# Wider dilated values, matmuls of one width in groups, an earlier first norm, row loads held in their place and five more warm-up matmuls in an fp32 encoder block

## The chip, the cores and the metric

The kernel runs on one core of one Trainium2 chip. The metric is the device time of one execution in microseconds (us). A core has a matmul engine (TensorE, PE in the profile; PEld is its weight load), two engines for elementwise work (VectorE, DVE; ScalarE, ACT), GpSimd (POOL), SyncE (SP) whose queue issues most transfers, and 16 DMA engines. Matmuls write eight accumulation banks of 128 partitions by 512 floats.

## The reference, cut to what matters

One encoder block over 256 tokens of width 2048, all in fp32:

```python
h = rms_norm(x, attn_norm)
qa, ka, va, qb, kb, vb, ga, gb = split(h @ w_in)           # A: 8 query heads, 2 key/value heads; B: 12 heads in 3 groups
ya = windowed_gqa(qa, ka, va, rel_bias_table, sink_a)       # |i-j| <= 128, a sink logit per head
yb = dilated_attention(qb, kb, vb, rel_bias_table)          # dilations 1, 4, 16; the groups merged by their denominators
merged = sigmoid(ga) * (ya @ w_branch_a) + sigmoid(gb) * (yb @ w_branch_b)
x = x + merged @ w_out
hf = rms_norm(x, ffn_norm)
g = dwconv_centred(hf @ w_ffn_gate, conv_w, conv_b)         # depthwise, width 3
x = x + (gelu(g) * (hf @ w_ffn_up)) @ w_ffn_down            # width 5632
x = x + sigmoid(rms_norm(x, ple_norm) @ w_ple_gate) * (p @ w_ple_proj)
return rms_norm(x, final_norm)
```

## The kernel before

**Precision.** Every matmul operand is held as a high and a low half (type fp32r). ACT writes a weight unit's high half (`uh`, L261, a copy that rounds), DVE its low half (`ul`, L262, the rest). The product is high x high, high x low and low x high. An activation tile such as `hs` (normed input) or `hf` (input of the MLP) holds per 128 channels a row of 512: 256 tokens high, 256 tokens low.

**Weights.** They come in pieces of 1 MB (`raw`, three buffers, SP's queue, L241). A piece is two units of 1024 columns, eight blocks of 128 x 128 each; six units of `uh` and `ul` exist. `drop` gives a unit back and `pump` then orders the next one's copies.

**Products.** Where the weights stand still in the array (`block`), one block costs a pair of matmuls: L289, the high half against all 512 columns, and L290, the low half against the 256 high columns, adding to the upper half of the same bank:

```python
nc.tensor.matmul(acc, hi[:, w], m, start=first, stop=False, skip_group_check=True)
nc.tensor.matmul(acc[:, T:], lo[:, w], m[:, :T], start=False, stop=last, skip_group_check=True)
```

`product` runs 16 such pairs, over 16 chunks of channels. Values must come with tokens on the partitions, so `value_product` has the activation stand still and the weights move: L312, L313, L314 per chunk and token half, over as many columns as heads are done at once (two heads: 256). All later stages but the MLP's first half (gates, branches, output, down projection, embedding) move 512 columns of weights, three matmuls at a time (L324 to L326), many in a Strassen form over "S" pieces.

**Order.** `_plan` lists the projections. The first seven (two keys, five queries of A) run interleaved, chunk by chunk, while weights and input arrive. Then come A's values (job FIRST = 7), three queries, and for each of four `j`: near values (dilation 1, two heads, every second `j`), three keys, far values (two heads), three queries. `at` hangs small work on (job, step) and `run_due` emits it in front of that step: with job i the last query of an attention block, scores at (i+1, 9), transposes at (i+2, 11 or 12), weighted values at (i+3, 4). The scores take the key and query tiles `kf`, `qf`, and for far heads `k`, `q` (L712). A compiler's scheduler orders the instructions of each engine from this program; `keep` fixes an instruction's place.

**The norm.** The projections work on the input without its norm; `rms` hangs up the sums of squares (L429), the root on DVE and POOL (L435, L437), the diagonal `rdg` (L444) and its broadcast by PE (L450), and everything behind a projection (`after`) multiplies by it. A second such norm stands in the MLP's first half.

**Start and rows.** Before the first product PE multiplies constants (`WARM` = 9). In the output projection's first stage, `D0`, the kernel loads the residual's rows `xr` (four loads of 0.5 MB, L870, on SP's queue) and transposes the last `merged` chunks (L812).

**The MLP.** Two halves, `E0` and `E1`, of 44 products each, gate and up in turn; the first four of `E0` run jointly. In `E0`, steps 2 to 5 transpose the residual into `hf`.

## Time and profile before

| | |
|---|---|
| median of 3 runs | 1474.07 us (1472.39 to 1474.58) |
| the profiled execution | 1474.83 us, of which the program's span is 1473.0 |
| PE busy | 1456.9 us, 7766 matmuls |
| PE weight load busy | 1247.8 us |
| DVE busy | 1241.5 us |
| ACT busy | 810.5 us |
| DMA | 282.93 MB, mean 192 GB/s |
| granted PE clock over the span | 0.998 |

A row of the timeline has start, duration, engine, source line, operation, output <- inputs, shape, count, and in brackets the idle time before it and what ended that. A row of the table by stretches has the stretch, its length, then for each engine the busy time with the number of instructions in brackets, the granted PE clock, the DMA share and GB/s. A matmul's duration reaches over the start of the next one, since matmuls are pipelined: what one costs in a stream is the distance between starts.

### The profile page before, as it was taken

How to read it: one execution, taken by the hardware profiler on the slowest of the kernel's cores; microseconds unless marked ns; L12 is line 12 of the kernel's file. 1: busy time of each engine (PE TensorE's matmuls, PEld its weight loads, DVE VectorE, ACT ScalarE, POOL GpSimd, SP SyncE). 2: the span in 40 equal slices, each digit the busy share in tenths (PEclk: the TensorE clock that was granted, in tenths of full speed). 3: DMA queues.
4: the chain of work that ended last, by engine and by line, in shares of the span. 5: the costliest groups of instructions: out<-in, count | busy, mean ns of one | idle time of the engine just before them, and what ended most of it. 6: DMA issues, size and time to landing. Idle time of an engine off the chain costs nothing.

```text
span 1473.0 us, 20121 instructions
## 1 busy us (share of the span) xinstructions
PE 1456.9 (99%) x7766; PEld 1247.8 (85%) x7766; DVE 1241.5 (84%) x1841; ACT 810.5 (55%) x1153; POOL 4.8 (0%) x9
## 2 busy tenths in 40 slices
PE   9999999999999999999999999999999999999997
PEld 8899999988888887888888888888888888888785
DVE  7587665669989989989888899988888889999994
ACT  7466444446555555565555556454555555555763
POOL 0000000000000000000000000000000000000000
PEclk9999999999999999999999999999999999999999
DMA  9654454445456456464555545465545455446462
GB/s 318 236 199 144 154 184 178 160 155 200 172 200 229 169 211 248 155 234 185 199 183 189 201 152 219 181 248 176 196 176 196 178 194 179 184 188 232 168 222 93
DMA packets 46460, 282.93 MB, mean 192 GB/s; under 512 B 5076, under 2 KB 9812, under 8 KB 14108
## 3 DMA queue, kind: packets, MB, share of 16 engines
q1 hardware_dynamic: 45356, 280.20, 52.1%
q10 hardware_dynamic: 1008, 1.45, 0.3%
q8 instruction: 61, 1.00, 0.3%
q14 instruction: 35, 0.29, 0.1%
HBM read 279.49 MB, written 2.14 MB: 191 GB/s over the span
## 4 chain that ended last, share of the span: by engine, by line
PE 91%; DVE 4%; DMA 2%; ACT 1%; issue 1%; POOL 0%; POOLq 0%; ACTq 0%
PE bank L289 31%; PE bank L290 15%; PE bank L324 12%; PE bank L325 12%; PE bank L326 12%; DMA raw<-in_wts 2%; PE bank L312 2%; PE bank L313 2%; PE bank L314 2%; DVE ul L262 1%; DVE vl L262 1%; ACT uh L261 1%; PE bank L812 1%; PE bank L635 0%; PE bank L582 0%
## 5 line engine op out<-in xcount | busy, mean ns | idle before, releaser
L261 ACT ACTIVATE uh<-raw 128x1024 fp32r<-128x1024 f32 (+2 forms) x518 | 522.6, 1017 | 493.1 <-PE bank L289 272.0
L262 DVE TENSOR_TENSOR ul<-raw,uh 128x1024 fp32r<-128x1024 f32 (+2 forms) x518 | 601.0, 1171 | 184.4 <-ACT uh L261 181.8
L289 PE MATMUL bank<-hf,uh 128*128 128x512 f32 x1408 | 493.6, 397 | 0.0
L290 PE MATMUL bank<-hf,ul 128*128 128x256 f32 x1408 | 393.4, 280 | 0.0
L289 PEld LDWEIGHTS bank<-hf,uh 128*128 128x128 f32 x1408 | 264.6, 188 | 63.1
L290 PEld LDWEIGHTS bank<-hf,ul 128*128 128x128 f32 x1408 | 265.7, 189 | 0.2
L289 PE MATMUL bank<-hs,uh 128*128 128x512 f32 x544 | 195.9, 402 | 2.1 <-DVE hs L422 2.1
L290 PE MATMUL bank<-hs,ul 128*128 128x256 f32 x544 | 153.5, 283 | 0.0
L261 ACT ACTIVATE vh<-raw 128x1024 fp32r<-128x1024 f32 x92 | 97.4, 1058 | 59.9 <-DVE raw L254 28.3
L289 PEld LDWEIGHTS bank<-hs,uh 128*128 128x128 f32 x544 | 103.5, 190 | 25.0 <-DVE hs L422 2.4
L262 DVE TENSOR_TENSOR vl<-raw,vh 128x1024 fp32r<-128x1024 f32 x92 | 112.2, 1221 | 0.5 <-ACT vh L261 0.2
L290 PEld LDWEIGHTS bank<-hs,ul 128*128 128x128 f32 x544 | 104.3, 192 | 0.1
L324 PE MATMUL bank<-uh,act 128*128 128x512 f32 x232 | 90.8, 391 | 0.0
L325 PE MATMUL bank<-ul,act 128*128 128x512 f32 x232 | 90.7, 391 | 0.0
L326 PE MATMUL bank<-uh,act 128*128 128x512 f32 x232 | 90.7, 391 | 0.0
L324 PE MATMUL bank<-uh,hs 128*128 128x512 f32 x172 | 67.6, 393 | 0.0
L326 PE MATMUL bank<-uh,hs 128*128 128x512 f32 x172 | 67.5, 392 | 0.0
L325 PE MATMUL bank<-ul,hs 128*128 128x512 f32 x172 | 67.3, 391 | 0.0
L312 PE MATMUL bank<-uh,hs 128*128 128x256 f32 x224 | 63.8, 285 | 0.0
L313 PE MATMUL bank<-ul,hs 128*128 128x256 f32 x224 | 63.5, 283 | 0.0
L314 PE MATMUL bank<-uh,hs 128*128 128x256 f32 x224 | 63.4, 283 | 0.0
L254 DVE TENSOR_TENSOR raw<-raw 128x1024 f32<-128x1024 f32 x46 | 56.2, 1222 | 0.5
(236 smaller groups left out, 2232.4 us busy)
## 6 DMA issues: line engine op xcount, KB each, us to landing
raw<-in_wts SPq DMA_DIRECT2D x251, 1024.0 KB, 4.8
raw<-in_wts SPq DMA_DIRECT2D x12, 512.0 KB, 6.7
xr<-in_xrow SPq DMA_DIRECT2D x4, 512.0 KB, 9.8
x<-in_xt SPq DMA_DIRECT2D x13, 128.0 KB, 5.8
hb<-hold SPq DMA_DIRECT2D x3, 514.0 KB, 7.6
hb<-hold SPq DMA_DIRECT2D x2, 768.0 KB, 6.6
last<-in_gainrow SPq DMA_DIRECT2D x1, 1024.0 KB, 4.8
out<-xr SPq DMA_DIRECT2D x4, 256.0 KB, 2.6
```

The costliest lines, as they stand in the source:

```text
L254: nc.vector.tensor_tensor(raw[:, :2 * WIDE], raw[:, WIDE:3 * WIDE], raw[:, :2 * WIDE], op=ALU.subtract)
L261: nc.scalar.activation(hi, src, AF.Copy)
L262: nc.vector.tensor_tensor(lo, src, hi.bitcast(F32), op=ALU.subtract)
L289: nc.tensor.matmul(acc, hi[:, w], m, start=first, stop=False, skip_group_check=True)
L290: nc.tensor.matmul(acc[:, T:], lo[:, w], m[:, :T], start=False, stop=last, skip_group_check=True)
L312: nc.tensor.matmul(acc[:, :T], xh, hi, start=(k == 0), stop=False)
L313: nc.tensor.matmul(acc[:, :T], xh, lo, start=False, stop=False)
L314: nc.tensor.matmul(acc[:, :T], xl, hi, start=False, stop=(k == KC - 1))
L324: nc.tensor.matmul(acc, sh, wh, start=first, stop=False)
L325: nc.tensor.matmul(acc, sh, wl, start=False, stop=False)
L326: nc.tensor.matmul(acc, sl, wh, start=False, stop=last)
L812: nc.tensor.transpose(p[:, k, t * P:(t + 1) * P], src(t)[:, k * P:(k + 1) * P], ident)
```

## The change

It does the following.

- Values of B: near values of all four heads in one product, far values of two `j` (four heads) in one product: 512 moving columns instead of 256. A's values stay at 256.
- Products behind the first seven take two units at a time: all high matmuls of the sixteen blocks, then all low ones (`unit_blocks`, `JOINED`). Work hung on a step is emitted among the high ones.
- The first norm's sums at step 4 and its broadcast at step 10 of A's values, instead of steps 6 and 12 of the query product behind.
- `WARM` 14 instead of 9.
- The four row loads keep their place in the program.
- `yb` becomes four tiles, whose room holds the far values first and part of the MLP's activations later; some small tiles have one buffer, `tb` shares one, `rd` is padded to 32 columns.

Line numbers of the changed kernel are higher: L289 and L290 are L305 and L309 in grouped products (L291 and L292 in the first seven), L261 and L262 are L263 and L264, L312 to L314 are L343 to L345, L581 to L583 are L612 to L614, L870 is L907.

PE, the query product behind A's values and the first scores (`bank` an accumulation bank, `uh`, `ul` a unit's halves). Before, the end of the product and the scores' start:

```order
L289 MATMUL bank_757<-hs_98,uh_582 128x512
L290 MATMUL bank_757<-hs_98,ul_583 128x256
L289 MATMUL bank_757<-hs_98,uh_610 128x512
L290 MATMUL bank_757<-hs_98,ul_611 128x256
L581 MATMUL bank_788<-kf_722,qf_730 128x256
L582 MATMUL bank_788<-kf_722,qf_730 128x256
```

And now:

```order
L309 MATMUL bank_693<-hs_102,ul_524 128x256 x8
L309 MATMUL bank_693<-hs_102,ul_528 128x256 x8
L305 MATMUL bank_761<-hs_102,uh_586 128x512 x8
L305 MATMUL bank_761<-hs_102,uh_626 128x512
L612 MATMUL bank_777<-kf_707,qf_715 128x256
L613 MATMUL bank_777<-kf_707,qf_715 128x256
L614 MATMUL bank_777<-kf_707,qf_715 128x256
```

The scores still stand in front of step 9, now behind nine high matmuls instead of nine pairs.

DVE, from the gathering of the first products (`first`) to the norm's root (`rv`). Before:

```order
L549 TENSOR_TENSOR rows_529<-bank_527,mk_102 20x512
L411 SCALAR_TENSOR_TENSOR first_534<-bank_148,t_535 128x256
L411 SCALAR_TENSOR_TENSOR first_538<-bank_149,t_539 128x256
L262 TENSOR_TENSOR ul_583<-raw_507,uh_582 128x1024
L411 SCALAR_TENSOR_TENSOR first_542<-bank_150,t_543 128x256
L411 SCALAR_TENSOR_TENSOR first_546<-bank_151,t_547 128x256
L262 TENSOR_TENSOR ul_611<-raw_507,uh_610 128x1024
L411 SCALAR_TENSOR_TENSOR first_550<-bank_152,t_551 128x256
L262 TENSOR_TENSOR ul_642<-raw_517,uh_641 128x1024
L262 TENSOR_TENSOR ul_670<-raw_517,uh_669 128x1024
L435 TENSOR_SCALAR rv_691<-bank_686 128x4
```

And now:

```order
L580 TENSOR_TENSOR rows_533<-bank_531,mk_105 20x512
L442 SCALAR_TENSOR_TENSOR first_538<-bank_152,t_539 128x256
L442 SCALAR_TENSOR_TENSOR first_542<-bank_153,t_543 128x256
L264 TENSOR_TENSOR ul_587<-raw_511,uh_586 128x1024
L442 SCALAR_TENSOR_TENSOR first_546<-bank_154,t_547 128x256
L442 SCALAR_TENSOR_TENSOR first_550<-bank_155,t_551 128x256
L466 TENSOR_SCALAR rv_595<-bank_590 128x4
```

The root stands behind four of the scaled gathers and one unit, before it stood behind all five and four units.

SP, the row loads among the weight loads. Before:

```order
L241 DMA raw_5108<-in_wts 128x2048
L870 DMA xr_5211<-in_xrow 128x2x512 x2
L241 DMA raw_5153<-in_wts 128x2048
L241 DMA raw_5191<-in_wts 128x2048
L870 DMA xr_5211<-in_xrow 128x2x512 x2
```

And now, five weight pieces later:

```order
L243 DMA raw_5062<-in_wts 128x2048
L907 DMA xr_4920<-in_xrow 128x2x512
L243 DMA raw_5097<-in_wts 128x2048
L907 DMA xr_4920<-in_xrow 128x2x512
L243 DMA raw_5140<-in_wts 128x2048
```

The four loads went out in two pairs; they now alternate with weight loads.

The diff, cut:

```diff
@@ -71,12 +71,13 @@
     for h in range(FIRST - KVH, QH):
         project("q", h, QA + h)
     for j in range(HG):
-        if j % 2 == 0:
-            jobs.append(("v", (KVH + j, KVH + j + 1), (VB + j, VB + j + 1)))
+        if j == 0:
+            jobs.append(("v", tuple(KVH + i for i in range(HG)), tuple(VB + i for i in range(HG))))
         for g in range(NG):
             project("k", KVH + g * HG + j, KB + g * HG + j)
-        far = [g * HG + j for g in range(1, NG)]
-        jobs.append(("v", tuple(KVH + i for i in far), tuple(VB + i for i in far)))
+        if j % 2 == 0:
+            far = [g * HG + j + i for i in range(2) for g in range(1, NG)]
+            jobs.append(("v", tuple(KVH + i for i in far), tuple(VB + i for i in far)))
         for g in range(NG):
             project("q", QH + g * HG + j, QB + g * HG + j)
     return jobs
...
@@ -84,8 +85,9 @@
 
 FIRST = 7
 START = FIRST + 1
-WARM = 9
+WARM = 14
 JOINT = 4
+JOINED = 2
 WIDE = 2 * T
 _JOBS = _plan()
 NA = len(_JOBS)
...
@@ -292,28 +294,57 @@
         if o == _LAST_OF[u]:
             drop(u)
 
+    def unit_blocks(todo):
+
+        ends, units = [], []
+        for _ in range(JOINED):
+            u = _FBLOCKS[state["at"] + len(ends)][0]
+            units.append(u)
+            for o in range(_LAST_OF[u] + 1):
+                acc, m, first, last = next(todo)
+                nc.tensor.matmul(acc, weights(u)[0][:, o * P:(o + 1) * P], m,
+                                 start=first, stop=False, skip_group_check=True)
+                ends.append((acc, m, last, u, o))
+        for acc, m, last, u, o in ends:
+            nc.tensor.matmul(acc[:, T:], weights(u)[1][:, o * P:(o + 1) * P], m[:, :T],
+                             start=False, stop=last, skip_group_check=True)
+            if o == _LAST_OF[u]:
+                drop(u)
+        state["at"] += len(ends)
+
+    def products(i, moving, n, accs):
+
+        def todo():
+            for k in range(n):
+                run_due(i, k)
+                for acc in accs:
+                    yield acc, moving(k), k == 0, k == n - 1
+
+        blocks, end = todo(), state["at"] + n * len(accs)
+        while state["at"] < end:
+            unit_blocks(blocks)
+        assert next(blocks, None) is None
+
     def product(i, moving, n, ring):
         acc = bank(ring)
-        for k in range(n):
-            run_due(i, k)
-            block(acc, moving(k), k == 0, k == n - 1)
+        products(i, moving, n, [acc])
         return acc
 
-    def value_product(i, paired):
+    def value_product(i, paired, n):
 
         accs = [bank("acc") for _ in range(2)]
         for k in range(KC):
             run_due(i, k)
             u, o = _FBLOCKS[state["at"]]
-            hi, lo = (w[:, o * P:(o + 2) * P] for w in weights(u))
+            hi, lo = (w[:, o * P:(o + n) * P] for w in weights(u))
             for t, acc in enumerate(accs):
                 tokens = (TWINS if paired else HALVES)[t]
                 xh, xl = (hs[:, k, c:c + T][:, tokens] for c in (0, T))
-                nc.tensor.matmul(acc[:, :T], xh, hi, start=(k == 0), stop=False)
-                nc.tensor.matmul(acc[:, :T], xh, lo, start=False, stop=False)
-                nc.tensor.matmul(acc[:, :T], xl, hi, start=False, stop=(k == KC - 1))
-            state["at"] += 2
-            if o + 1 == _LAST_OF[u]:
+                nc.tensor.matmul(acc[:, :n * P], xh, hi, start=(k == 0), stop=False)
+                nc.tensor.matmul(acc[:, :n * P], xh, lo, start=False, stop=False)
+                nc.tensor.matmul(acc[:, :n * P], xl, hi, start=False, stop=(k == KC - 1))
+            state["at"] += n
+            if o + n - 1 == _LAST_OF[u]:
                 drop(u)
         return accs
...
     att = ExitStack()
     ap_ = att.enter_context(tc.tile_pool(name="att", bufs=2))
     ya = big.tile([P, QH, 2 * T], FR, name="ya")
-    yb = big.tile([P, HG, 2 * T], FR, name="yb")
+    yb = {}
     hs = big.tile([P, KC, 2 * T], FR, name="hs", tag="R0")
...
-    tb = sc.tile([NBUCK, NH], F32, name="tb", bufs=1)
     mk = ap_.tile([NH, 2 * T], F32, name="mk", tag="s1", bufs=2)
+    tb = ap_.tile([NBUCK, NH], F32, name="tb", tag="k", bufs=7)
...
-        q = ap_.tile([P, 4, T], F32, name="sq4", tag="v", bufs=2) if c else squares
...
+        q = ap_.tile([P, 4, T], F32, name="sq4", tag="v%d" % (2 + c % 2 * 2), bufs=1) if c else squares
...
-        rd = ap_.tile([P, 2], F32, name="rd")
-        nc.vector.reciprocal(rd, den)
+        rd = ap_.tile([P, 32], F32, name="rd")
+        nc.vector.reciprocal(rd[:, :2], den)
...
-        row = ya[:, y] if y < QH else yb[:, y - QH]
+        if y >= QH:
+            yb[y - QH] = big.tile([P, 2 * T], FR, name="yb", tag="yb%d" % (y - QH))
+        row = ya[:, y] if y < QH else yb[y - QH]
...
+            w = len(n) * P
             if near:
-                v = ap_.tile([P, 2, 2, T], FR, name="v", bufs=2)
+                v = ap_.tile([P, 2, 2, w], FR, name="v", tag="v%d" % len(n), bufs=1)
             else:
-                v = ap_.tile([P, 2, T], F32, name="vf", bufs=2)
+                j = (n[0] - KVH) % HG
+                v = [big.tile([P, 2, T], F32, name="vf", tag="yb%d" % (j + i)) for i in range(2)]
...
-                a, r = acc[t][:, :T], rc[0][:, c:c + 1]
+                a, r = acc[t][:, :w], rc[0][:, c:c + 1]
...
-                    nc.scalar.activation(v[:, t], a, AF.Copy, scale=r)
+                    for i in range(2):
+                        nc.scalar.activation(v[i][:, t], a[:, i * T:(i + 1) * T], AF.Copy, scale=r)
...
-                    vs[h].append((v[:, t, 0, c], v[:, t, 1, c]) if near else v[:, t, c])
+                    vs[h].append((v[:, t, 0, c], v[:, t, 1, c]) if near else
+                                 v[e // 2][:, t, e % 2 * P:(e % 2 + 1) * P])
...
         if i == FIRST:
-            rms([(START, 6), (START, 12)], tot, 0, HALVES + TWINS)
+            rms([(FIRST, 4), (FIRST, 10)], tot, 0, HALVES + TWINS)
             for c, (h0, h) in enumerate([(0, 4), (4, 4), (8, 4), (12, 4), (16, 4)]):
                 at(((FIRST, 8), (START + 1, 8), (START + 3, 8), (START + 5, 8), (START + 7, 8))[c], bias, h0, h)
         if kind == "v":
-            acc = value_product(i, n[0] >= KVH + HG)
+            acc = value_product(i, n[0] >= KVH + HG, len(n))
         else:
             acc = product(i, lambda k: hs[:, k, :], KC, "acc")
...
-        for half, (stage, y, names) in enumerate((("ba%d" % j, ya, ("M1", "M6")), ("bb%d" % j, yb, ("M7", "M5")))):
-            accs = wide_stage(stage, lambda k: y[:, k, :], names)
+        for half, (stage, y, names) in enumerate((("ba%d" % j, lambda k: ya[:, k, :], ("M1", "M6")), ("bb%d" % j, yb.get, ("M7", "M5")))):
+            accs = wide_stage(stage, y, names)
...
     def load_rows(n):
-        nc.sync.dma_start(xr[:, :, cut[n]], xrow[:, :, cut[n]])
+        keep(nc.sync.dma_start(xr[:, :, cut[n]], xrow[:, :, cut[n]]))
...
-                       big.tile([P, 4, 2 * T], FR, name="act1", tag="yb"),
+                       [big.tile([P, 2 * T], FR, name="act1", tag="yb%d" % i) for i in range(4)],
...
-        for k in range(KC if joint else 0):
-            run_due(stage, k)
-            for a in accs:
-                block(a, hf[:, k, :], k == 0, k == KC - 1)
+        if joint:
+            products(stage, lambda k: hf[:, k, :], KC, accs)
```

More of the change, by code (lines that the diff above doesn't have):

```diff
@@ L830, in halved @@
     def halved(r):
-        h = sc.tile([P, 2], F32, name="rh")
+        h = sc.tile([P, 2], F32, name="rh", bufs=1)
         nc.vector.tensor_scalar(h, r[:, :2], 0.5, None, op0=ALU.mult)
@@ L890, in rows_root @@
     def rows_root():
-        q = sc.tile([P, 2], F32, name="rs")
+        q = sc.tile([P, 2], F32, name="rs", bufs=1)
         nc.vector.tensor_tensor(q, held["ssq"][:, 0], held["ssq"][:, 1], op=ALU.add)
@@ L897, in _encoder @@
     at(("D0", 2, 4), combine, "merged", held["merged"], 6, 2)
-    held["ssq"] = sc.tile([P, 2, 2], F32, name="ssq")
+    held["ssq"] = sc.tile([P, 2, 2], F32, name="ssq", bufs=1)
     residual("D0", 0, lambda k: held["merged"][:, k, :], "merged", True)
@@ L913, in activation_row @@
         k %= FHALF
-        tile, k = (held["act"][0], k) if k < 16 else (held["act"][1], k - 16) if k < 20 else (held["act"][2], k - 20)
-        return tile[:, k, :]
+        return held["act"][1][k - 16] if 16 <= k < 20 else held["act"][k // 20 * 2][:, k - k // 20 * 20, :]
     def mlp(kind, n, acc):
@@ L968, in _encoder @@
                 nc.vector.tensor_tensor(pl_[k], pr[:, k], ph_[k].bitcast(F32), op=ALU.subtract)
-            held["ssq"] = sc.tile([P, 2, 2], F32, name="ssq")
+            held["ssq"] = sc.tile([P, 2, 2], F32, name="ssq", bufs=1)
         residual("F%d0" % half, 0, activation_row, "act", half)
```

## The prediction

> **What bounds the kernel now.** I read the page's head, then TensorE (PE) over chosen stretches, then the timeline at each place where PE stood idle.
>
> ```profile
> span 1473.0 us, 20121 instructions
> PE 1456.9 (99%) x7766; PEld 1247.8 (85%) x7766; DVE 1241.5 (84%) x1841; ACT 810.5 (55%) x1153; POOL 4.8 (0%) x9
> PE 91%; DVE 4%; DMA 2%; ACT 1%; issue 1%; POOL 0%; POOLq 0%; ACTq 0%
> ```
>
> PE is busy 99% of the span and carries 91% of the chain that ended last. Only two things can move the end: the spacing of matmuls, and the few places where PE waits. The profiled execution took 1474.83 us, 0.76 over the median of the runs (1474.07); I make the sum against it and then subtract 0.76.
>
> Spacing comes from stretches in which PE never pauses. An instruction is counted when any part of it lies in the stretch, so the spacing is (stretch + one duration) / count. The first three rows count the 512-wide half of the alternating pair (L289, one per pair); the last two count every matmul.
>
> ```profile
> 700.00:800.00 100.00, 100.00 (x290) 54.11 (x289) 1.00 0.53 190
> 1050.00:1150.00 100.00, 100.00 (x284) 53.26 (x283) 1.00 0.51 183
> 246.00:262.00 16.00, 16.00 (x47) 8.67 (x47) 1.00 0.47 175
> 235.00:245.00 10.00, 10.00 (x86) 1.00 0.44 151
> 535.00:545.00 10.00, 10.00 (x46) 1.00 0.32 125
> ```
>
> With 0.39 us for a 512-wide matmul and 0.28 for a 256-wide one: a pair costs 346.2 ns in the first half of the MLP (row 1), 353.5 in the second half, the same code (row 2), and 348.7 in the projections (row 3). A stream of 256-wide matmuls only (a value product) costs 119.5 each, a stream of 512-wide ones only (branch projection) 225.9. So an even stream would make 345.4 of a pair, and doubling the width of a matmul saves 2 x 119.5 - 225.9 = 13.1 ns.
>
> **Widened values.** Before, 6 of the 7 value products issue 96 matmuls of 256; now 3 issue 96 of 512. That is 576 removed, 288 added: 288 x 13.1 ns = 3.8 us off PE, all on the path. ACT and DVE empty the same number of elements in fewer instructions, under the next product; with two of three banks held, the product after that would be late first if they fell behind by 5.5 us. I take -3.8.
>
> The Trainium skill, "TensorE: Matmul & The Clock Gate", section "Back-to-back issue gap", gives a fixed cost of 2.5 ns per warm matmul. By it this term would be an estimated 288 x 2.5 ns = 0.7 us; the rows above show 13 ns, and they decide.
>
> **Grouped widths.** Products after the first seven now run sixteen 512-wide matmuls, then sixteen 256-wide ones. Nothing is added or removed; only the spacing can change. It applies to 704 pairs in each MLP half and to 27 x 16 = 432 pairs in the projections. One end: the even streams' 345.4 everywhere, giving 704 x (0.8 + 8.1) ns + 432 x 3.3 ns = 7.7 us saved. The other end is the one place where the present kernel runs four and four:
>
> ```profile
> 15.72 1.09 PE L289 MATMUL bank<-hs,uh 128*128 128x512 f32 x4
> 16.65 0.63 PE L290 MATMUL bank<-hs,ul 128*128 128x256 f32 x4
> 17.12 0.40 PE L289 MATMUL bank<-hs,uh 128*128 128x512 f32 x1
> ```
>
> (17.12 - 15.72) / 4 = 350 ns: at that price the first MLP half loses 2.7 us, the second wins 2.5, the projections lose 0.6: +0.8. The long streams are nearer to runs of sixteen than four matmuls in the loaded start, but the first MLP half shows that alternation can already reach 346. I take 347: +0.6 - 4.6 - 0.7 = -4.7.
>
> **Fourteen warm-ups.** Rows of PE at the start; the third counts the 512-wide halves (L289) from 7.36 to 13.25:
>
> ```profile
> 1.05 4.21 PE L223 MATMUL bank<-ones 128*128 128x128 f32 x18 [1.05 <-DVE mhalf L218]
> 7.36 0.80 PE L289 MATMUL bank<-hs,uh 128*128 128x512 f32 x1 [2.10 <-DVE hs L422]
> 7.36:13.25 5.89, 5.80 (x9) 3.11 (x10) 1.00 0.94 299
> 12.65 0.63 PE L289 MATMUL bank<-hs,uh 128*128 128x512 f32 x1
> 13.26 0.39 PE L289 MATMUL bank<-hs,uh 128*128 128x512 f32 x1
> 13.60 0.40 PE L289 MATMUL bank<-hs,uh 128*128 128x512 f32 x1
> 12.13 1.23 DVE L262 TENSOR_TENSOR ul<-raw,uh 128x1024 fp32r<-128x1024 f32 x1 [1.57 <-ACT uh L261]
> ```
>
> Nine warm-ups are 18 instructions, 4.21 us; then PE stands still for 2.1 us, and pairs cost up to 0.61 us until 13.26, where they fall to 0.34. So 4.2 us of work did not bring the full rate, 13.26 - 7.36 = 5.9 us did. Fourteen are 28 instructions, about 28 x 0.213 + 0.16 = 6.1 us, ending at 7.2, before the first product's operand allows 7.36: no delay, and the break closes. 5.9 us from 1.05 is 6.95, so I expect the full rate by 7.4. The stretch 7.36 to 13.26 holds nine pairs; at 0.347 they take 3.1, so at most 2.8 us are saved, and zero if the rate still comes at 13.3. The low halves of the fifth unit (last row) end at 13.36, while PE would want them at 7.36 + 16 x 0.347 + 0.23 = 13.1, so 0.3 goes back. I take -2.5.
>
> **First norm earlier.** Its sums move from the eighth product into the first value product, the broadcast (L450) from step 12 there to step 10 of the values. All its instructions move, their number stays: eight one-column matmuls and two of 256 on PE, the root's few on DVE, one on POOL, one copy on ACT. What it cures is one wait:
>
> ```profile
> 71.12 1.22 DVE L262 TENSOR_TENSOR ul<-raw,uh 128x1024 fp32r<-128x1024 f32 x1
> 72.25 0.42 DVE L417 TENSOR_TENSOR qf<-first,qf 128x256 fp32r<-128x256 f32 x1
> 72.73 0.39 PE L582 MATMUL bank<-kf,qf 128*128 128x256 f32 x1 [0.66 <-DVE qf L417]
> 65.07 1.02 POOL L437 TENSOR_TENSOR rr<-rv,mhalf 128x4 f32<-128x4 f32 x1 [64.63 <-DVE rv L435]
> 66.12 0.48 DVE L444 TENSOR_SCALAR rdg<-ident,rr 128x128 f32<-128x128 f32 x2 [1.13 <-POOL rr L437]
> 55.78 0.74 DVE L411 SCALAR_TENSOR_TENSOR first<-bank,t 128x256 f32<-128x256 f32 x2
> 50.08 0.39 PE L312 MATMUL bank<-uh,hs 128*128 128x256 f32 x1
> ```
>
> The first scores waited 0.66 us for a query that DVE finished late, behind a weight unit. With the norm some 10 us earlier this goes: -0.7. In its place the broadcast can wait: PE comes to step 10 at 50.08 + 10 x 6 x 0.1195 = 57.3 (this profile's clock). In the new DVE order the root stands behind four gathers that ended at 56.5 here; plus 0.2, POOL's 1.02 and the diagonal's 0.48 makes 58.2. Late by 0.9; by 0 if the units moved ahead of the gathers use DVE's idle time, by 3.4 if PE gains its 2.5 and DVE does not. I take +0.8.
>
> **Attention steps between the runs.** Scores, transposes and values keep their step numbers, but steps now go by at 0.227 us, not 0.347, with all sixteen low halves after them. Scores at step 9 come 9 x 0.12 = 1.1 us earlier after the query product. The tightest place:
>
> ```profile
> 152.36 1.06 ACT L261 ACTIVATE uh<-raw 128x1024 fp32r<-128x1024 f32 x1 [1.71 <-PE bank L289]
> 153.46 1.23 DVE L262 TENSOR_TENSOR ul<-raw,uh 128x1024 fp32r<-128x1024 f32 x1 [1.55 <-ACT uh L261]
> 155.05 0.64 DVE L712 TENSOR_TENSOR q<-u,rms 128x256 f32<-128x256 f32 x1
> 156.11 1.05 PE L600 MATMUL bank<-k,q 128*128 128x128 f32 x8
> ```
>
> The far query is ready at 155.69, 3.3 us after the product's last 512-wide matmul let ACT go (152.36); PE wants it at 156.11. PE would now come 1.1 earlier. But ACT's copy is released by the last high-half matmul, now 1.9 us before the product ends, so its 1.06 us leave the chain. The margin of 0.4 stays near 0.4; the transposes behind lose some 0.3. For about eight such places I take +0.8 in all, bounds 0 and 12 x 1.06.
>
> In the first MLP half the second norm's broadcast stands at a step that PE now reaches about 1 us earlier:
>
> ```profile
> 654.54 0.47 DVE L444 TENSOR_SCALAR rdg<-ident,rr 128x128 f32<-128x128 f32 x2
> 655.50 0.59 PE L450 MATMUL bank<-rdg,ones 128*128 128x256 f32 x2
> ```
>
> Ready at 655.0, used at 655.5: +0.5, bounds 0 and 1.7 (one more weight unit now stands ahead on DVE).
>
> **Held row loads.** Here the row loads (0.5 MB each) went out two by two, in front of weight loads on the same queue:
>
> ```profile
> 545.03 1.31 SPq L870 DMA_DIRECT2D xr<-in_xrow  x2
> 549.48 1.93 SPq L870 DMA_DIRECT2D xr<-in_xrow  x2
> 555.52 1.06 ACT L261 ACTIVATE uh<-raw 128x1024 fp32r<-128x1024 f32 x1 [3.92 <-DMA raw<-in_wts]
> 560.09 0.69 DVE L816 SCALAR_TENSOR_TENSOR merged<-bank,merged 128x512 fp32r<-128x512 f32 x1
> 560.83 0.66 PE L812 MATMUL bank<-ident,c 128*128 128x128 f32 x4 [1.69 <-DVE merged L816]
> ```
>
> ACT stood 3.92 us for a weight piece, DVE fell behind, and PE waited 1.69 us for the low half of `merged`. Now the four go out one at a time, five weight pieces later, with a weight load between each. Each puts the next weight load back by its issue, 1.31 / 2 = 0.7 us, and by 0.5 MB of transfer instead of 1; three piece buffers and six units cover that, and if they did not, ACT would stand again, one piece later. Two of the rows are needed at the end of this stage, some 40 us on. I take -1.6, bounds 0 (DVE late for another reason) and -2.0. The split of `yb`, the smaller buffers and the padded `rd` cost nothing: no instruction is added, PE covers them.
>
> **Sum.** -3.8 - 4.7 - 2.5 - 0.7 + 0.8 + 0.8 + 0.5 - 1.6 = -11.2. 1474.83 - 11.2 = 1463.6; against the median, 1462.9.
>
> **Rivals.** First, the spacing does not improve and the full rate comes late: -3.8 - 0.7 + 2.1 - 1.6 + 0.8 = -3.2, 1470.9. For it: the four-and-four row. Against: the even streams.
>
> Second, attention waits: every one of twelve score blocks comes 1.06 us too early because ACT or DVE has other work in front: 12.7 instead of 0.8, so 1474.8, within the noise. For it: the 0.4 us margin. Against: ACT's earlier release, and most other queries are ready long before.
>
> Third, the slow side: each 256-wide matmul in a run waits for its own weight load, and a pair costs more than alternating ones. Without grouping the sum is -6.5; the 1840 pairs average 349.6 ns now, so the gain is gone at 353.1 ns and a loss over 0.2% (2.9 us) begins at 354.7; at 356 the time is 1479.4. For it: alternation hides a load behind a 512-wide matmul every second time. Against: eight 128-wide matmuls with a load each took 1.05 us (row L600 above), about 111 ns apart, less than the value stream's 119.5, which loads for every matmul too. The Trainium skill, same page, "LDWEIGHTS (loading the stationary operand)", puts 128 columns at 107 ns; that would leave the run free, as these rows do.
>
> **How the numbers follow.** 0.2% of 1474 is 2.9 us, about what a measurement of this kernel can tell from no change. My forecast, with its terms inside their bounds: 0.74, from 1457 (all terms at their good ends) to 1468. First rival 0.12, mostly still faster, up to 1472. Second 0.09, third 0.05. So faster 0.85, same 0.09, slower 0.06. The range 1456 to 1470 leaves out most of the second and third and the weak end of the first.
>
> **What would show it.** Right: the second MLP half at about 347 ns per pair like the first; PE's full rate by 7.5 us; no PE wait above 1 us near 550; 288 value matmuls at 226. Wrong: new idle time of PE in front of scores, transposes or the two broadcasts, or pairs above 352 ns.

## The result: 1464.5 us, 0.6% faster, and the profile after

| | before | after |
|---|---|---|
| median (range, runs) | 1473.09 us (1472.39 to 1474.58, 6) | 1464.53 us (1461.98 to 1466.81, 6) |
| ratio of the runs | | 0.9939, 95% interval 0.9926 to 0.9952 |
| profiled execution / its span | 1474.83 / 1473.0 us | 1462.99 / 1461.2 us |

The kernel is 8.6 us faster in the median; the two profiled executions lie 11.8 apart, since that of before was 1.7 slower than its median and that of after 1.5 faster. The head of the page after:

```profile
span 1461.2 us, 19529 instructions
PE 1446.7 (99%) x7488; PEld 1235.3 (85%) x7488; DVE 1248.4 (85%) x1839; ACT 824.8 (56%) x1151; POOL 4.9 (0%) x9
PE 94%; DVE 2%; DMA 1%; ACT 1%; issue 1%; POOLq 0%; POOL 0%; ACTq 0%
```

278 matmuls fewer (288 for the values, less ten instructions of warm-up), and PE's share of the chain that ended last rose from 91 to 94%. The time is found by cutting both executions at the same matmuls. Columns: stretch in us from the span's start, its length, PE's busy time with the instructions, granted clock, DMA share, GB/s. Before: values and projections of A and B; gates and branches; first half of the MLP (gate and up products); its down product; second half; its down product up to the embedding's part.

```profile
50.08:311.77 261.69, 261.04 (x1783) 1.00 0.51 180
311.77:550.28 238.51, 238.51 (x1077) 1.00 0.51 191
638.42:884.74 246.32, 246.32 (x1428) 1.00 0.53 190
884.74:998.58 113.84, 113.84 (x501) 1.00 0.55 209
998.58:1247.31 248.73, 248.73 (x1410) 1.00 0.52 184
1247.31:1363.51 116.20, 116.20 (x516) 1.00 0.55 208
```

After, the same six:

```profile
47.49:305.36 257.87, 257.87 (x1496) 1.00 0.50 180
305.36:542.72 237.36, 237.36 (x1077) 1.00 0.50 188
628.47:875.76 247.29, 247.29 (x1428) 1.00 0.52 189
875.76:988.70 112.94, 112.94 (x500) 1.00 0.57 210
988.70:1233.61 244.91, 244.91 (x1409) 1.00 0.52 187
1233.61:1352.89 119.28, 116.62 (x516) 1.00 0.55 205
```

The starts and ends of these rows give every step of the profiled pair:

| part | moved by, us | the prediction had |
|---|---|---|
| start to the first values (50.08, now 47.49) | -2.6 | -2.5 |
| values and projections | -3.8 | -3.6 in sum |
| gates and branches | -1.2 | 0 |
| output projection (88.14, now 85.75) | -2.4 | -1.6 |
| first MLP half | +1.0 | +1.1 |
| its down product | -0.9 | 0 |
| second MLP half | -3.8 | -4.6 |
| its down product | **+3.1** | 0 |
| embedding's part, to the end | -1.3 | 0 |

The steps add to -11.9, within rounding the difference of the spans. Four parts moved that the sum did not touch. The largest has PE waiting: 119.28 us long, 116.62 busy. All engines' timeline of after at its start, cut to the rows that matter (bracket: idle time before, and what ended it):

```profile
1232.70 0.34 ACTq L998 DMA_DIRECT2D pair<-in_pt  x1
1239.56 0.72 ACT L1001 ACTIVATE t<-pair 128x256 fp32r<-128x256 f32 x2 [3.40 <-DMA pair<-in_pt]
1240.01 0.43 DVE L1002 TENSOR_TENSOR u<-pair,t 128x256 fp32r<-128x256 f32 x1 [3.40 <-ACT t L1001]
1241.36 1.22 DVE L256 TENSOR_TENSOR raw<-raw 128x1024 f32<-128x1024 f32 x1
1245.84 0.50 PE L356 MATMUL bank<-vl,S 128*128 128x512 f32 x1 [0.94 <-DVE vl L264]
1247.60 0.51 PE L355 MATMUL bank<-vh,S 128*128 128x512 f32 x1 [0.31 <-ACT vh L263]
1297.87 0.33 PE L849 MATMUL bank<-ident,xr 128*128 128x128 f32 x1 [0.66 <-DVE xr L915]
```

ACT issues the load of `pt` (the embedding's input, 256 KB, into a tile `pair`) and 3.5 us later wants it. It landed 6.8 us after its issue; ACT stood 3.40 us, DVE stood behind ACT, the Strassen combinations on `raw` (L256) came late, and PE ran dry three times (0.94, 0.31 and, ahead of 1248.86, 0.75 us). The last row is another wait of the same stage, for DVE's sum into `xr`, 50 us later; E4 shows that it stays when the first three are gone. In the profile of before (answer for the line of the load: count, durations in ns, first and last start; then the time to landing) it landed 2.2 us sooner after its issue, and nobody waited:

```profile
L964 ACTq DMA_DIRECT2D pair<-in_pt x1: 335/335/335, 1244.6 to 1244.6; - x1
...
DMA to landing us min/median/max: 4.6/4.6/4.6
```

Where the prediction looked, the norm and the scores stand without a wait:

```profile
54.85 0.48 DVE L475 TENSOR_SCALAR rdg<-ident,rr 128x128 f32<-128x128 f32 x2 [0.66 <-POOL rr L468]
55.71 0.59 PE L481 MATMUL bank<-rdg,ones 128*128 128x256 f32 x2
68.08 0.28 PE L612 MATMUL bank<-kf,qf 128*128 128x256 f32 x1
```

### The profile page after: what moved, and what is told of

Its sections match the earlier page's. It is cut to its first block, busy times and chain, and to the rows that moved or that the text cites. A ratio compares the mean times of both kernels' runs of the same rounds, so it can differ in the third digit from the quotient of the medians.

```text
span 1461.2 us, 19529 instructions
## 1 busy us (share of the span) xinstructions
PE 1446.7 (99%) x7488; PEld 1235.3 (85%) x7488; DVE 1248.4 (85%) x1839; ACT 824.8 (56%) x1151; POOL 4.9 (0%) x9
## 4 chain that ended last, share of the span: by engine, by line
PE 94%; DVE 2%; DMA 1%; ACT 1%; issue 1%; POOLq 0%; POOL 0%; ACTq 0%
PE bank L305 29%; PE bank L309 15%; PE bank L356 13%; PE bank L355 13%; PE bank L357 13%; PE bank L343 2%; PE bank L345 2%; PE bank L344 2%; PE bank L291 2%; PE bank L292 1%; DVE ul L264 1%; PE bank L849 1%; PE bank L666 0%; DMA pair<-in_pt 0%; DMA raw<-in_wts 0%
## 5 line engine op out<-in xcount | busy, mean ns | idle before, releaser
L263 ACT ACTIVATE uh<-raw 128x1024 fp32r<-128x1024 f32 (+2 forms) x518 | 521.8, 1017 | 397.9 <-PE bank L305 190.3
L264 DVE TENSOR_TENSOR ul<-raw,uh 128x1024 fp32r<-128x1024 f32 (+2 forms) x518 | 595.8, 1168 | 152.6 <-ACT uh L263 72.0
L305 PE MATMUL bank<-hf,uh 128*128 128x512 f32 x1408 | 336.5, 391 | 0.0
L305 PEld LDWEIGHTS bank<-hf,uh 128*128 128x128 f32 x1408 | 258.6, 188 | 50.1
L309 PEld LDWEIGHTS bank<-hf,ul 128*128 128x128 f32 x1408 | 180.6, 191 | 6.9
L309 PE MATMUL bank<-hf,ul 128*128 128x256 f32 x1408 | 183.0, 283 | 0.0
L263 ACT ACTIVATE vh<-raw 128x1024 fp32r<-128x1024 f32 x92 | 97.5, 1059 | 66.9 <-DVE raw L256 36.7
L264 DVE TENSOR_TENSOR vl<-raw,vh 128x1024 fp32r<-128x1024 f32 x92 | 111.8, 1217 | 0.4
L305 PE MATMUL bank<-hs,uh 128*128 128x512 f32 x432 | 109.2, 395 | 0.0
L305 PEld LDWEIGHTS bank<-hs,uh 128*128 128x128 f32 x432 | 77.7, 189 | 13.8
L436 ACT ACTIVATE t<-bank 128x256 f32<-128x256 f32 x122 | 46.4, 383 | 75.5 <-PE bank L309 70.1
L309 PEld LDWEIGHTS bank<-hs,ul 128*128 128x128 f32 x432 | 55.4, 191 | 2.2
L256 DVE TENSOR_TENSOR raw<-raw 128x1024 f32<-128x1024 f32 x46 | 56.1, 1219 | 0.6
L356 PE MATMUL bank<-vl,S 128*128 128x512 f32 x138 | 54.4, 394 | 1.8 <-DVE vl L264 1.7
L309 PE MATMUL bank<-hs,ul 128*128 128x256 f32 x432 | 56.0, 282 | 0.0
L355 PE MATMUL bank<-vh,S 128*128 128x512 f32 x138 | 54.5, 399 | 0.3 <-ACT vh L263 0.3
```

Of the source, the lines that this page charges most:

```text
L256: nc.vector.tensor_tensor(raw[:, :2 * WIDE], raw[:, WIDE:3 * WIDE], raw[:, :2 * WIDE], op=ALU.subtract)
L263: nc.scalar.activation(hi, src, AF.Copy)
L264: nc.vector.tensor_tensor(lo, src, hi.bitcast(F32), op=ALU.subtract)
L305: nc.tensor.matmul(acc, weights(u)[0][:, o * P:(o + 1) * P], m, start=first, stop=False, skip_group_check=True)
L309: nc.tensor.matmul(acc[:, T:], weights(u)[1][:, o * P:(o + 1) * P], m[:, :T], start=False, stop=last, skip_group_check=True)
L355: nc.tensor.matmul(acc, sh, wh, start=first, stop=False)
```

## The experiments

Twelve kernels, on three chips; the kernel before has medians of 1472.74 (beside E1 to E4), 1472.66 (E5 to E8) and 1472.76 us (E9 to E12) there. A stage's length in a profile repeats to 0.2 us, mostly to 0.05, between executions of kernels that agree in it, while a ratio to before has an interval of 1.3 to 2 us on either side; so both are used.

**E1: before with fourteen warm-ups.** `-WARM = 9` / `+WARM = 14`

> The kernel before, with 14 matmuls on constants in place of 9 and nothing else. Theory: the granted clock is full by about 5.6 us of the span in place of 13.2, the first values product starts about 2.6 us earlier (47.5 in place of 50.1), and nothing downstream gives it back: -2.6 us against before (1470.5, ratio 0.998). Rival 1: the seven joint products then wait for their loads and splits, and gain under 1 us. Rival 2: the slow spacing of the second half's gate and up products (353.3 ns a pair in the profiled run of before, 346.2 in the first half) is not a property of the program but of one execution: then this run shows 346 to 348 there and gains another 4 to 5 us in that stage. Theory: 353 plus or minus 1 again, and 346 plus or minus 1 in the first half.

Measured: 1471.41 against 1472.74, ratio 0.9992 (0.9983 to 1.0001): -1.3 us, about half the price; the interval reaches 0. The halves of the MLP repeat their lengths of before, 246.3 and 248.7, so the two spacings belong to the program (rival 2 falls). Its profiled execution, 1476.12, was the slowest of eleven, and shows in the kernel **before** what was found above:

```profile
14.13 0.38 PE L290 MATMUL bank<-hs,ul 128*128 128x256 f32 x1 [0.77 <-DVE ul L262]
1250.52 0.42 ACT L967 ACTIVATE t<-pair 128x256 fp32r<-128x256 f32 x1 [3.15 <-DMA pair<-in_pt]
1260.07 0.55 PE L325 MATMUL bank<-vl,S 128*128 128x512 f32 x1 [1.81 <-DVE vl L262]
```

ACT waits 3.15 us for `pt` here too, so this wait is a matter of the execution as well as of the change. The first row is what rival 1 named, though the gain is not under its 1 us: a product waits for the low halves of its weights.

**E2: the changed kernel without grouping.**

```diff
-        while state["at"] < end:
-            unit_blocks(blocks)
+        for step in todo():
+            block(*step)
```

> The changed kernel with the grouping undone: each product again issues a 512-wide and a 256-wide matmul in turn; all else stays. Theory (the gain of the second half comes from the grouping): the pair goes from 347.8 to about 353.3 ns in the second half (704 pairs, +3.9 us), from 348.9 to 346.5 in the first (704 pairs, -1.7), and the projections from 347 to 348.7 (+0.5). The wait on the transfer of pt at the start of the second half's down product (+3.1 us in the changed kernel) comes from the earlier end of that stage's ACT and DVE work under grouping, so it goes away with it: together about 0 (1464, plus or minus 1.5). Rival: that wait belongs to where the transfer is issued, grouped or not: then it stays, and the time is about +2.7 (1467). Rival 2: the second half runs at 347 to 348 also in turn, the spacing came from elsewhere: then -1.5 or less (1463).

Measured: 1467.39, ratio 0.9960 (0.9948 to 0.9972), +2.9 on after. Both halves, by stretch:

```profile
629.17:879.90 250.73, 250.73 (x1428) 1.00 0.52 188
992.80:1241.53 248.73, 248.73 (x1409) 1.00 0.51 184
```

The second half is back at 248.73 to the digit, as the theory had it: 248.73 / 704 = 353.3 ns a pair. The first is not at 246.3 but at 250.73, 4.4 us or 6.3 ns a pair above before, so it runs at the slow spacing too: there the expectation failed, and rival 2 with it. The `pt` wait shrank to 0.2 us of ACT, and the down product took 115.54, so that part of the theory held. The first rival's time, 1467, came out, but not by its cause, since the wait did not stay. With these tiles grouping is worth 3.4 + 3.8 us in the two halves.

**E3: the changed kernel with 256-wide value matmuls,** same tiles and banks.

```diff
-                nc.tensor.matmul(acc[:, :n * P], xh, hi, ...)      # and two more
+                for c in range(0, n * P, T):
+                    s = slice(c, c + T)
+                    nc.tensor.matmul(acc[:, s], xh, hi[:, s], ...)  # and two more
```

> The changed kernel with each of the 288 value matmuls of 512 columns issued as two of 256 over the same tiles and banks; all else stays. Theory from the profile after: a 512-wide value matmul took 232 ns, two of 256 wide 239: +7 ns x 288 = +2.0 us (1466.5). The prediction's term: 13.1 ns x 288 = +3.8 us (1468.3). Rival: the wide matmuls are bound by their weights' split, and the narrow ones fit the same time: 0. By the Trainium skill's page TensorE: Matmul & The Clock Gate, section Back-to-back issue gap, an estimate from its 2.5 ns would be +0.7 us.

Measured: 1464.99, ratio 0.9948 (0.9934 to 0.9961): +0.5, with the stage 2.4 longer and the `pt` wait shorter (ACT 2.7 us, the down product 117.88). Inconclusive in the median; E7 repeats it without the wait.

**E4: `pt` loaded 30 us earlier,** into the tile `cmb`, free by then.

```diff
             mlp(kind, n, product(stage, lambda k: hf[:, k, :], KC, "e"))
+            if half and (kind, n % FHALF) == ("u", 17):
+                pr = held["tok"].tile([P, 4, P], F32, name="cmb")
+                pr = pr.rearrange(...)
+                nc.scalar.dma_start(pr, pt)
-            pr = held["tok"].tile([P, 2, T], F32, name="pair", bufs=2)
-            nc.scalar.dma_start(pr, pt)
```

> The changed kernel with the transfer of pt issued about 12 us earlier, into a tile that is free by then; its two copies and subtractions stay where they are. Theory: the stall at the start of the second half's down product comes from this transfer (issued at 1232.7, landed 6.8 us later, ACT idle 3.40 us for it, DVE idle 3.40 us for ACT, and then PE 1.10 + 0.48 + 1.03 + 0.82 us over its usual spacing): ACT's idle time there goes to 0, the stage loses 2.5 to 3.4 us, and so does the kernel (1461.5, ratio to before about 0.992). Rival: VectorE is behind at this place anyway, since the subtractions on the raw weights queue behind the last up product; then ACT's wait moves to the raw weights and under 1 us is gained.

Measured: **1461.17** (1460.73 to 1461.72), ratio 0.9919 (0.9906 to 0.9931): -3.4 on after, and the runs lie within 1 us instead of 5. (The issue came at 1202, 30 us ahead, not the 12 of the expectation.) The load, the second copy, and the down product:

```profile
1202.21 0.33 ACTq L999 DMA_DIRECT2D cmb<-in_pt  x1
1237.57 0.42 ACT L1003 ACTIVATE t<-cmb 128x256 fp32r<-128x256 f32 x1 [0.58 <-DVE pair L440]
1234.48:1351.01 116.53, 115.72 (x517) 1.00 0.54 206
```

Nobody waits for the load; the stage lost 2.75 us. The load is shown to cause that much of the +3.1; the wait for `xr` stays, 0.81 us here. (The kernel before was 0.35 us faster beside this run than beside that of after, so against it the gain is about 3.0.)

**E5: four transposes later.** PE still stood 0.81 us in E4 before the first transpose in the last down product. `-(("F11", 0, 2), ("F11", 0, 5), ("F11", 1, 0), ("F11", 1, 3))` / `+(("F11", 0, 4), ("F11", 1, 0), ("F11", 1, 2), ("F11", 1, 5))`

> The run with the early transfer of pt, and besides the four first turns of the second half's last down product placed two or so groups of three matmuls later. In the run with the early transfer TensorE still stood 1.20 us at 1294.8 in front of the first of them, for VectorE's sum into xr. Theory: the sum is done 1.1 us after TensorE asked, so a later place takes 0.8 to 1.0 us away: 1460.3 against 1461.2 (ratio to before 0.991). Rival: the pl rows are then late for the combination that reads them, and the wait comes back there: 0.

Measured: **1460.08** (1459.95 to 1460.69), ratio 0.9917 (0.9903 to 0.9930). The wait fell to 0.53 us only, and a new one of 0.58 stands where the next transposes begin:

```profile
1294.96 0.33 PE L849 MATMUL bank<-ident,xr 128*128 128x128 f32 x1 [0.53 <-DVE xr L915]
1355.58 0.33 PE L849 MATMUL bank<-ident,xr 128*128 128x128 f32 x1 [0.58 <-DVE xr L915]
```

The down product is 0.85 us shorter than in E4 and the part behind it 0.5 longer, so most came back, as the rival said; the rest of the 1.1 us lies ahead of the first values (47.37 in place of 48.40), where the twelve profiles with fourteen warm-ups spread over 1.2 us anyway. This is the lowest median of the study (E12's is 0.2 above), and the base of the seven runs below.

**E6: the base with nine warm-ups.** `-WARM = 14` / `+WARM = 9`

> The kernel of the run before this one (early pt, later turns) with 9 matmuls on constants in place of 14. It no longer has the pt wait, whose length differs from run to run, so that the 14 are weighed more finely than on the kernel before (-1.3 us, interval about -2.5 to +0.1). Theory (the clock alone): +2.5 us. Rival (the first products wait for loads and splits when they run at full rate: 0.5 to 1.2 us at 12.8 us of the span in two of the runs, absent in the others): +1.2 to +1.7.

Measured: 1460.66 (1460.31 to 1460.72), ratio 0.9919 (0.9906 to 0.9933), against the base's 1460.08 (1459.95 to 1460.69): +0.6, with ranges that overlap. Less than even the rival. In the profiles the first values start 1.47 us later than in the base (48.84 against 47.37), and the last down product is 0.78 shorter (114.90 against 115.68), so part of the start's loss was won back there. PE's stretches at the start of E6, from its first product on:

```profile
7.21:8.37 1.16, 1.16 (x7) 1.00 1.11 309
8.37:11.53 3.16, 3.16 (x13) 0.51 0.91 287
11.53:13.26 1.73, 1.73 (x10) 0.92 0.83 259
```

Nine warm-ups do not always cost what they cost in the profile of before (half rate by the spacing of its pairs from 7.36 to 13.26; the clock column reads 1.00 there): here the first pairs ran at the full clock, and half rate lasted 3.2 us.

**E7: the base with 256-wide value matmuls** (the edit of E3).

> The same base (early pt, later turns) with each of the 288 value matmuls of 512 columns issued as two of 256. On the changed kernel this cost +2.4 us in the stage that holds them by the profile, but only +0.5 in the median, since the pt wait was shorter in that run. Theory: on a base without that wait the median moves by the stage: +2.4 (8.4 ns x 288). The prediction's term was 3.8. Rival: +0.5 is the true price.

Measured: 1462.87 (1462.61 to 1463.67), ratio 0.9936 (0.9924 to 0.9949): +2.8. The values' and projections' stretch:

```profile
47.69:308.00 260.31, 260.31 (x1783) 1.00 0.50 178
```

The base has 257.84 there: 2.47 us / 288 = 8.6 ns for each matmul, neither 13.1 nor 2.5. The theory held.

**E8: the base, row loads not held.** `-keep(nc.sync.dma_start(xr...))` / `+nc.sync.dma_start(xr...)`

> The same base with the four row loads no longer held in program order: only SP's queue changes (five weight loads fewer stand ahead of the first row load). Theory: SP's order alone makes the wait of 2.08 us ahead of the merged turns in the first output product, so it comes back: +1.7 to +2.4 (the stage lost 2.38 under the change). Rival: that wait came from the older place of the whole program in time, and the loads' order alone does nothing: within 0.5.

Measured: 1461.93 (1461.18 to 1462.12), ratio 0.9929 (0.9915 to 0.9942): +1.9. The loads leave two by two again, ACT starves for weights, and PE waits for `merged`:

```profile
537.91 1.31 SPq L907 DMA_DIRECT2D xr<-in_xrow  x2
547.84 1.06 ACT L263 ACTIVATE uh<-raw 128x1024 fp32r<-128x1024 f32 x1 [3.36 <-DMA raw<-in_wts]
553.15 0.55 PE L849 MATMUL bank<-ident,c 128*128 128x128 f32 x3 [1.18 <-DVE merged L853]
```

The order on SP's queue alone makes the wait.

**E9: the base with the small tiles as before.** No instruction changes place; only addresses do.

```diff
-    tb = ap_.tile([NBUCK, NH], F32, name="tb", tag="k", bufs=7)
+    tb = sc.tile([NBUCK, NH], F32, name="tb", bufs=1)
-        rd = ap_.tile([P, 32], F32, name="rd")
+        rd = ap_.tile([P, 2], F32, name="rd")
-    name="rh", bufs=1   name="rs", bufs=1   name="ssq", bufs=1
+    name="rh"           name="rs"           name="ssq"
```

> The kernel with early pt and later turns, with the five small tiles as in the kernel before (table beside the sums' tiles, two buffers for rh, rs and ssq, rd of 2 columns). Every engine's instructions stand in the same order; only places in the on-chip memory move: t, u and the other tiles of that pool by 96 bytes, the pool of the later stages (pair, S, vh, vl, c) by 192. Theory: these places are what made the matmuls of the gates, the first down product and the last products 226.8 in place of 228.6 ns; then about -1.0, -0.9 and -0.9 us come back there: +2.0 to +2.8. Rival 1 (the prediction: small tiles cost nothing): within 0.5. Rival 2: the place of hs, hf and pl did it: within 0.5 here, and the next run shows it.

Measured: **1463.77** (1463.33 to 1463.83), ratio 0.9937 (0.9923 to 0.9950): +3.7. Gates and branches, then the first down product:

```profile
305.87:544.43 238.56, 238.56 (x1076) 1.00 0.50 187
878.03:991.87 113.84, 113.84 (x501) 1.00 0.56 209
```

These are the lengths of before (238.51, 113.84), where the base has 237.52 and 112.96. PE's groups by line in that down product (after the bar: busy us, mean ns of one; then idle time), E9:

```profile
L356 PE MATMUL bank<-ul,act 128*128 128x512 f32 x116 | 45.3, 390 | 0.0
L356 PE MATMUL bank<-vl,S 128*128 128x512 f32 x30 | 11.7, 391 | 0.0
L356 PE MATMUL bank<-vl,act 128*128 128x512 f32 x10 | 4.0, 397 | 0.0
L355 PE MATMUL bank<-uh,S 128*128 128x512 f32 x10 | 4.0, 397 | 0.0
```

And the base:

```profile
L356 PE MATMUL bank<-ul,act 128*128 128x512 f32 x116 | 45.1, 389 | 0.0
L356 PE MATMUL bank<-vl,S 128*128 128x512 f32 x30 | 11.7, 389 | 0.0
L356 PE MATMUL bank<-vl,act 128*128 128x512 f32 x10 | 3.9, 390 | 0.0
L355 PE MATMUL bank<-uh,S 128*128 128x512 f32 x10 | 3.9, 389 | 0.0
```

These are four of the twelve groups. Six groups, 60 matmuls, take one operand from the pool that moved by 192 bytes (`vh`, `vl`, `S`) and the other mostly from outside it (`act`, `uh`, `ul`): in the base all six stand at 389 or 390 ns, in E9 they pay 2 to 9 ns each. That makes some 0.4 of the stage's 0.88 us; the many others pay 1 to 2 ns. (The byte counts come from the tiles' sizes; a trace prints no addresses.) By stage E9 loses 1.0 us in the gates, 0.9 in this product, 0.7 in the last down product and 0.5 each in the output projection and near the end. The tiles, priced at nothing, are worth 3.7 us.

**E10: the base with `hs`, `hf`, `pl` at the places of before.** Ahead of `hs`: `+for i in range(HG): nc.gpsimd.memset(big.tile([P, 2 * T], F32, name="first_yb", tag="yb%d" % i)[:, :1], 0.0)`

> The same base with hs, hf and pl back at their places of the kernel before (the four yb tiles are laid out ahead of them, with four one-column fills on GpSimd; nothing else changes). Theory (the small tiles' places made the faster matmuls): within 0.5, and 226.8 ns in the first down product. Rival: the place of hs, hf and pl made them: +2.0 to +2.8, with 228.6 ns in the first down product and 229.5 in the branch stages.

Measured: 1460.54 (1460.27 to 1460.76), ratio 0.9915 (0.9902 to 0.9929): +0.5, and the down product at 112.98. The place that the split of `yb` gave to these tiles is worth about half a microsecond; the profile has it in the output projection, 86.36 us against 85.84. Theory held.

**E11: the base in turn, with both sets of places of before** (edits of E2, E9 and E10).

> The same base with the grouping undone and both sets of places of the kernel before. With new places the products in turn ran at 353 ns a pair in both halves (250.6 and 248.6 us of stage), in the kernel before at 346.2 in the first half (246.2) and 353.3 in the second (248.6). Theory: the places choose the spacing of products in turn: the first half is back at 246.2, the second at 248.6, and the three other stages at their times of before; about 1466 in sum. Rival: the order of the instructions ahead chooses it (the values are 512 wide now): then the first half stays at 250.6.

Measured: 1466.95 (1465.83 to 1467.19), ratio 0.9957 (0.9944 to 0.9969). The two halves:

```profile
631.23:877.57 246.34, 246.34 (x1427) 1.00 0.52 189
991.42:1240.15 248.73, 248.73 (x1410) 1.00 0.51 185
```

246.34 and 248.73: to 0.02 us the kernel before, although the order ahead of them is another. Up to the end of the first half PE, DVE and ACT run the same instructions in the same order as in E2, which had 250.73. The places choose the spacing of matmuls in turn; which of the two sets does it was not tried.

**E12: the base with the late norm.** `-rms([(FIRST, 4), (FIRST, 10)]...` / `+rms([(START, 6), (START, 12)]...`

> The same base with the first norm at the kernel before's places, during the product after the first values. The prediction had -0.7 for the wait ahead of the first scores that goes, and +0.8 for a new wait at the broadcast, of which the profile after shows none. Theory: the wait of 0.8 us ahead of the first scores comes back, and nothing is won elsewhere: +0.7. Rival: within 0.3, the earlier norm hides nothing that PE feels.

Measured: 1460.26 (1459.95 to 1461.34), ratio 0.9915 (0.9901 to 0.9928): +0.2; the stretch is 258.15 against 257.84 long, with 0.05 us of PE idle. Neither the wait nor the gain of 0.7 is there on this base; the rival held.

## Why the prediction was right, and where it was not

The total was right (1462.9 forecast, 1464.53 measured), but in part by luck: two terms of over 3 us were absent from the sum, and they nearly cancel. The terms that it did have measure -9.0 together, against the -11.2 forecast. Measured prices, from the medians of E4 and E6 to E9 and E12 and, for grouping, from the stretches:

| term | forecast | measured |
|---|---|---|
| widened values | -3.8 | -2.8 (E7) |
| grouped widths | -4.7 | -3.5: +1.0, -3.8, and -0.65 in the projections (E11's stretch of 258.49 less 257.84; with the new places E2 has only 258.04) |
| fourteen warm-ups | -2.5 | -0.6 (E6), -1.3 (E1) |
| first norm, both sides | +0.1 | -0.2 (E12) |
| attention steps, second broadcast | +1.3 | no wait found; the broadcast lies in grouping's +1.0 |
| held row loads | -1.6 | -1.9 (E8) |
| `yb`, small tiles | 0 | -3.7 (E9), place of `hs` up to -0.5 (E10) |
| wait for `pt` | none | +3.4 (E4; 2.75 by the stage) |

With E6's price the column makes -9.3, and -9.8 with E10's; measured -8.6.

**Widened values:** right mechanism, size off. The step took 225.9 ns, the price of a branch projection's stream, for a 512-wide value matmul, and its sign of being right was 226. In the trace of the base the starts of these matmuls lie 232 ns apart, those of E7's 256-wide ones 120: some 8 ns for each, as E7's 8.6. One stream's spacing does not hold for another.

**Grouped widths:** 347 everywhere was the choice; the halves show 247.29 / 704 = 351.3 with the transposes and the broadcast in it (before 349.9), and 347.9. The price stood within its bounds. What the step did not see is why two halves of the same code differed: E2 and E11 answer that in turn they run at the one spacing or the other by the tiles' places, and that grouping makes them indifferent to it: 244.9 us of second half and 247.3 of first in every grouped kernel here, E9 and E10 with their old places among them. Against the places of before the first half loses 1.0, against the new ones it wins 3.4.

The first rival (no better spacing, a late full rate) falls: the second half gains 3.8, and the full rate was there at PE's first product (7.09).

**Fourteen warm-ups:** in the profiled pair the step came out to the letter (-2.6). It failed in taking the profiled execution for the rule. E6 shows a milder one, and E1, E4 and E9 show 0.3 to 0.8 us of waiting for low halves at full rate, the 0.3 that the step gave back.

**First norm, attention:** the broadcast's operand was ready at 55.3, not 58.2, since the four gathers ahead of the root were done at 53.6, not 56.5; PE came at 55.71. The second rival (twelve late score blocks) is false: in after PE waits ahead of no score. So is the third (a run bound by its weight loads): of the 347.9 ns of a pair the 512-wide matmul takes 228.5 and the 256-wide one 119.5, by the starts in the trace of after, no more than in the value stream before.

**Held loads:** right, with mechanism and size.

**Small tiles:** "no instruction is added, PE covers them" was the step that failed. It counted instructions; the price was in the matmuls, whose operands the small tiles move in memory. E9 explains the gates and the first down product, which the sum had at 0, and 0.5 of the 1.3 at the end.

**The omitted wait:** the list of places where PE waited came from one execution of before, in which the load of `pt` landed just in time: ACT took it up at 1249.27, within 0.1 us of its landing (1244.6 + 4.6). Two things add up in the wait. With matmuls in turn ACT wanted the tile 4.7 us after the issue (before, E1, E2), with grouping 3.5 (after, E3), 1.2 us sooner. And the load landed after 4.6, 7.8, 4.9, 6.8 and 6.3 us in these five executions. So some 1.2 of the 3.4 us come of the change, the rest of the landing time; what makes a landing long was not tried.

## What to carry to other kernels

Read the profile also for transfers that land just in time: a load issued from a compute engine's queue a few microseconds ahead of its use is a wait that the next improvement, or the next execution, will pay; issue it as soon as its room is free. An edit that only moves tiles in memory is an edit of the matmuls that read them: before a gain or a loss is put down to an instruction, run the same instructions at the old places. And when a sum of terms meets the measured total, cut both executions at the same instructions and compare part by part; here two errors of over 3 us had cancelled by chance.

## What the hardware showed that was not expected

- **Places.** With the order of every engine unchanged, moving one pool by 192 bytes and another by 96 made the matmuls of a stage 0.8% slower (113.84 against 112.96 us), those with operands from both sides of the move 2 to 9 ns each. The Trainium skill, "SBUF — State Buffer", section "SBUF: two separate sides", says that the matmul engine never waits for anyone at its port; this case's E9 differs from its base in places alone, and the matmuls do differ. What in the memory makes it was not tried.
- **Spacing in turn.** 704 pairs of a 512-wide and a 256-wide matmul in turn took 246.3 or 250.7 us in the first half, by the tiles' places, and 248.7 in the second with either (before, E1, E2, E11). By the starts in the traces the longer spacing lies mostly in the 512-wide matmul: 232.5 ns in the first half of before, 236.9 in that of E2.
- **The clock after a pause.** In E1's profiled execution PE stood idle 1.81 us ahead of 1260.07, for the reason above. PE's stretches ahead of it and behind it:

```profile
1250.00:1257.50 7.50, 7.50 (x34) 1.00 0.02 4
1260.60:1264.00 3.40, 3.40 (x10) 0.53 0.86 364
1264.00:1268.00 4.00, 4.00 (x19) 1.00 0.44 182
```

  The granted clock fell from 1.00 to 0.53 for 3.4 us, ten instructions in place of 15: the pause cost about as much again as it lasted. In after, shorter pauses in the same place (0.94 and 0.31 us in the rows above) left the clock of the stage at 1.00, and so did the pause of 1.69 us ahead of 560.83 in before. In the clock records of the traces the changes lie 3.41 us apart: full at 5.00, half at 8.41 and full at 11.82 in E6, half at 1260.40 and full at 1263.81 in E1. So what a pause costs may hang on where it falls in such a stretch; no experiment moved a pause, and this stays open.
